# Lower halves of every second weight chunk made by accumulating DMAs from GpSimd instead of VectorE subtractions

## Chip, core and metric

One core of one Trainium2 chip. The metric is the time of one execution in microseconds (us), device time, as the median of several runs. The engines are named TensorE (PE), VectorE (DVE), ScalarE (ACT), GpSimd (POOL) and SyncE (SP).

## What is computed

Two transformer-like blocks on one sequence of 512 tokens, 1024 wide, in float32. The first block has two layers, each with a convolution branch, a retention branch and a windowed attention branch; the second has a spatial gate, a gated linear recurrence and a feed-forward part:

```python
def reference(x, ...):
    x = first_block(x, ...)                 # 2 x hybrid_layer
    return second_block(x, ...)

def hybrid_layer(x, ...):
    h = rms_norm(x, norm_g)
    z = h @ w_in
    y_conv = conv_module(...) @ w_conv_out
    y_ret = retention_branch(...) @ w_ret_out
    y_attn = window_attention_branch(...) @ w_attn_out
    merged = g[:, :, 0] * y_conv + g[:, :, 1] * y_ret + g[:, :, 2] * y_attn
    return x + merged @ w_out

# at the end of second_block
hid = silu(h1 @ w_ffn_gate) * (h1 @ w_ffn_up)
ffn = hid @ w_ffn_down
h = layer_norm(ALPHA * h1 + ffn + ple, ...)
```

Nearly all of the arithmetic is products of activations with weight matrices.

## The kernel before

Every product with a weight matrix is made of three: each operand is split into an upper part `hi` (rounded to the fp32r type that PE reads) and a lower part `lo`, the float32 value less its upper part. `mm3` (lines 173 to 177) then adds up upper times upper, upper times lower and lower times upper in one PSUM tile, so one block of 128x128 weights costs three matmuls, on lines 175, 176 and 177. In the products that hold the weights still (`fm`, line 179) the weights' lower part is first read by the third of the three.

The weights lie in DRAM in the order in which they are used, in 502 chunks of 128x1024 float32 (512 KB, 8 blocks each; `w`, `NCHUNK`). `take` (line 158) hands out the blocks. Before it hands out a block of chunk c it has everything up to chunk c+2 split (`WB` = 3, line 162). For each chunk `_split_next` (line 135) writes three steps into the program:

- the chunk's load into a tile `raw`, issued by SP (`_load_raw`, line 131),
- its upper part, a cast `hi<-raw` on ACT (line 152; the first three chunks on line 150),
- its lower part, a subtraction `lo<-raw,hi` on DVE (line 153),

and then the load of the next chunk, three ahead. `raw`, `hi` and `lo` each have three buffers that go round. So the cast for chunk c waits until PE has read the last block of chunk c-3 out of `hi`, the lower part until PE has read `lo` of chunk c-3, and the load of chunk c+3 until the lower part of chunk c is made, which is the last to read `raw`. ACT, DVE, SP and PE take their instructions in the order of the program; that order is set by a scheduler when the program is built.

Eleven chunks in `HOLD` (306 to 311 and 399 to 403) go another way: they are split into slots of their own, by `split` (line 206) on lines 208 and 209.

Most chunks serve matmuls of 512 columns. In two places they serve less. The down projection of the feed-forward part, at the end of the program, runs over the two halves of the tokens, one after the other (`HALVES`, lines 1306 to 1317), 256 columns each, and takes its 44 chunks (458 to 501) for 22 x 8 blocks twice. The first projection of the second block (`tmproj` with `halves`, lines 961 and 191) takes chunks 312 to 319 for two token tiles at a time.

Steps that the text names: the feed-forward part (lines 1296 to 1303) evicts with a tanh on ACT (line 1299, recorded on line 226) and two operations on DVE (line 216), and splits the product on lines 208 and 209.

Of the kernel before, what the change touches and what calls it, by code (L numbers as in the profile page):

```python
# [10 lines left out]
F32 = mybir.dt.float32  # L11
F32R = mybir.dt.float32r
I32 = mybir.dt.int32
AF = mybir.ActivationFunctionType
ALU = mybir.AluOpType
# [55 lines left out]
class Kern:  # L71
# [63 lines left out]
    def _split_next(self):  # L135
        c = self.nsplit
        if c >= NCHUNK:
            return
        while self.nraw <= c:
            self._load_raw()  # L140
        raw = self.raw.pop(c)
        if c in HOLD:
            parts = [self.split(raw[:, i * 512:i * 512 + 512]) for i in range(2)]
            self.hi[c], self.lo[c] = [x[0] for x in parts], [x[1] for x in parts]
        else:
            h = self.hp.tile([128, 1024], F32R, tag="hi", name=f"hi{c}")
            l = self.lp.tile([128, 1024], F32R, tag="lo", name=f"lo{c}")
            if c in self.first:
                with self.tc.issue_after(self.first[c].ins):
                    self.A.copy(h, raw)  # L150
            else:
                self.A.copy(h, raw)  # L152
            self.V.tensor_tensor(out=l, in0=raw, in1=h.bitcast(F32), op=ALU.subtract)  # L153
            self.hi[c], self.lo[c] = h, l
        self.nsplit += 1
        self._load_raw()
# [1362 lines left out]
```

## Time and profile before

| what | value |
|---|---|
| median of 2 runs | 3081.85 us (3081.53 to 3082.16) |
| the profiled execution | 3081.39 us |
| its span, first to last instruction | 3079.6 us |
| granted TensorE clock, mean | 0.997 |
| PE / PEld / DVE / ACT / POOL busy | 98% / 82% / 69% / 38% / 0% |
| DMA moved | 281.77 MB, 28.0% of the 16 DMA engines on the queue of SP |

Busy time is the time in which an engine runs an instruction; matmuls are pipelined, so a busy PE need not run at its peak. PEld are the weight loads of PE, which run beside its matmuls. DMAs are issued by an engine's sequencer and carried by 16 DMA engines; "to landing" is from the issue to the update of the semaphore that tells of it. In a timeline row the first number is the start in us from the span's start, the second the duration in us, and in brackets stands how long the engine sat idle before it, and what released it.

### The profile page before, as it was taken

Reading aid. Unit: us, or ns where it says so; the run is one execution under the profiler, and the core shown is the slowest. Engines: PE = TensorE matmul, PEld = TensorE weight load, DVE = VectorE, ACT = ScalarE, POOL = GpSimd, SP = SyncE. Lnnn points to the kernel's source line nnn. Section 1 sums busy time; section 2 is a strip of 40 time slices with the busy share of each in tenths; the row PEclk is TensorE's granted clock in tenths of the full one; section 3 lists DMA queues with packets and bytes.
Section 4 is the critical chain, followed back from the end, with each engine's and each line's share of the span. In section 5 each row is a group of like instructions: output and inputs, shape, how many; then the busy total and the mean of one; then the engine's idle time right before and its main releaser. Section 6 shows DMA issues by size and latency. Waiting matters only on the chain.

```text
span 3079.6 us, 37755 instructions
## 1 busy us (share of the span) xinstructions
PE 3033.3 (98%) x14728; PEld 2510.4 (82%) x14728; DVE 2128.3 (69%) x3934; ACT 1156.2 (38%) x1822; POOL 0.2 (0%) x4
## 2 busy tenths in 40 slices
PE   9999999999999999999999999999999999999998
PEld 7777888887888877788888788887888888788898
DVE  8687997877344677889787754388876656744356
ACT  5545223334233454532333423243543333322233
POOL 0000000000000000000000000000000000000000
PEclk9999999999999999999999999999999999999999
DMA  4121322221323322123222132333222223132354
GB/s 163 62 76 49 97 83 81 76 83 62 103 96 130 117 69 68 56 84 95 76 76 76 63 102 96 107 118 131 89 83 69 69 78 121 62 96 96 97 170 138
DMA packets 82114, 281.77 MB, mean 91 GB/s; under 512 B 9232, under 2 KB 11536, under 8 KB 81808
## 3 DMA queue, kind: packets, MB, share of 16 engines
q1 hardware_dynamic: 81936, 279.37, 28.0%
q8 instruction: 115, 1.88, 0.3%
q14 instruction: 63, 0.52, 0.1%
HBM read 275.14 MB, written 4.19 MB: 91 GB/s over the span
## 4 chain that ended last, share of the span: by engine, by line
PE 91%; DVE 6%; ACT 2%; issue 1%; DMA 0%; SPq 0%; ACTq 0%; DVEq 0%
PE pm L175 20%; PE pm L177 20%; PE pm L176 20%; PE pa L175 7%; PE pa L177 7%; PE pa L176 7%; DVE s L213 1%; PE pi L773 1%; PE pa L794 1%; DVE lo L153 1%; PE pi L175 1%; PE pi L177 1%; PE pi L176 1%; ACT s L226 1%; PE pa L1094 1%
## 5 line engine op out<-in xcount | busy, mean ns | idle before, releaser
L175 PE MATMUL pm<-s,hi 128*128 128x512 f32 x2912 | 1140.7, 392 | 1.8 <-ACT s L226 1.8
L176 PE MATMUL pm<-s,hi 128*128 128x512 f32 x2912 | 1139.5, 391 | 0.0
L177 PE MATMUL pm<-s,lo 128*128 128x512 f32 x2912 | 1135.9, 390 | 0.0
L152 ACT CAST hi<-raw 128x1024 fp32r<-128x1024 f32 x488 | 513.5, 1052 | 1365.9 <-PE pm L176 801.2
L153 DVE TENSOR_TENSOR lo<-raw,hi 128x1024 fp32r<-128x1024 f32 x491 | 599.8, 1222 | 450.2 <-ACT hi L152 442.4
L175 PEld LDWEIGHTS pm<-s,hi 128*128 128x128 f32 x2912 | 547.0, 188 | 119.3 <-issue 3.5
L177 PEld LDWEIGHTS pm<-s,lo 128*128 128x128 f32 x2912 | 547.2, 188 | 114.7 <-issue 2.2
L176 PEld LDWEIGHTS pm<-s,hi 128*128 128x128 f32 x2912 | 547.3, 188 | 113.0 <-issue 1.7
L216 DVE SCALAR_TENSOR_TENSOR s<-s,m,s 128x497 f32<-128x497 f32 (+14 forms) x480 | 356.3, 742 | 11.2
L216 DVE SCALAR_TENSOR_TENSOR s<-s,pm 128x512 f32<-128x512 f32 x186 | 127.2, 684 | 208.9 <-PE pm L177 208.5
L175 PE MATMUL pa<-hi,s 128*128 128x512 f32 x576 | 228.4, 397 | 11.7 <-ACT hi L150 6.7
L176 PE MATMUL pa<-lo,s 128*128 128x512 f32 x576 | 227.3, 395 | 0.0
L177 PE MATMUL pa<-hi,s 128*128 128x512 f32 x576 | 226.9, 394 | 0.0
L208 ACT CAST s<-s 128x512 fp32r<-128x512 f32 x192 | 115.6, 621 | 192.5 <-DVE s L216 146.7
L213 DVE TENSOR_TENSOR s<-s,s 128x512 f32<-128x512 f32 (+2 forms) x284 | 168.5, 610 | 3.2 <-ACT s L226 0.5
L209 DVE TENSOR_TENSOR s<-s,s 128x512 fp32r<-128x512 f32 x192 | 128.5, 687 | 28.7 <-ACT s L208 27.9
L175 PEld LDWEIGHTS pa<-hi,s 128*128 128x128 f32 x576 | 109.1, 190 | 36.4 <-ACT hi L150 6.7
L176 PEld LDWEIGHTS pa<-lo,s 128*128 128x128 f32 x576 | 109.2, 190 | 22.6 <-DVE lo L153 0.8
L177 PEld LDWEIGHTS pa<-hi,s 128*128 128x128 f32 x576 | 109.0, 189 | 22.0
L175 PE MATMUL pa<-s,hi 128*128 128x256 f32 (+1 forms) x408 | 122.2, 300 | 1.0 <-ACT s L1277 1.0
L177 PE MATMUL pa<-s,lo 128*128 128x256 f32 (+1 forms) x408 | 122.1, 300 | 0.0
L176 PE MATMUL pa<-s,hi 128*128 128x256 f32 (+1 forms) x408 | 121.5, 298 | 0.0
(143 smaller groups left out, 2905.1 us busy)
## 6 DMA issues: line engine op xcount, KB each, us to landing
raw<-w SPq DMA_DIRECT2D x502, 512.0 KB, 3.4
s<-xT SPq DMA_DIRECT2D x16, 256.0 KB, 5.3
xd<-s SPq DMA_DIRECT2D x8, 256.0 KB, 2.0
s<-xd SPq DMA_DIRECT2D x8, 256.0 KB, 4.8
out<-s SPq DMA_DIRECT2D x16, 128.0 KB, 1.8
ckt<-ck SPq DMA_DIRECT2D x1, 1344.0 KB, 6.4
s<-c_b_v SPq DMA_DIRECT2D x2, 256.0 KB, 3.9
s<-c_b_i SPq DMA_DIRECT2D x2, 256.0 KB, 3.9
```

The source lines that it names most:

```text
L152: self.A.copy(h, raw)
L153: self.V.tensor_tensor(out=l, in0=raw, in1=h.bitcast(F32), op=ALU.subtract)
L175: T.matmul(out, lhsT=lh, rhs=rh, start=start, stop=False)
L176: T.matmul(out, lhsT=lh, rhs=rl, start=False, stop=False)
L177: T.matmul(out, lhsT=ll, rhs=rh, start=False, stop=stop)
L208: self.A.copy(h, src)
L209: self.V.tensor_tensor(out=l, in0=src, in1=h.bitcast(F32), op=ALU.subtract)
L213: return self.V.tensor_tensor(out=out, in0=a, in1=b, op=op)
L216: return self.V.scalar_tensor_tensor(out=out, in0=a, scalar=s, in1=b, op0=op0, op1=op1)
L226: return self.A.activation(out, a, f, bias=bias, scale=scale, **kw)
L773: T.transpose(ps[:, i * 128:i * 128 + 128], pr[i][:, x * 128:x * 128 + 128], self.ck("ident"))
L794: T.matmul(ps[:, 0:w], lhsT=a[hs, ns], rhs=b[hs, j0:j1], start=first, stop=last)
```

## The change

For every odd chunk above 5 the subtraction on DVE goes. ACT writes the negated upper part into the tile `lo` (a copy with scale -1), and GpSimd then issues a DMA that adds `raw` to it in place: -hi + raw. Even chunks, chunks up to 5 and the held chunks stay as they are. There are 242 such odd chunks. Line numbers behind line 153 move on by five: what stood on line 153 is line 158 in the new file, the three matmuls are on 180, 181 and 182, `act` is on 231, and the new DMA is on 156.

```diff
             else:
                 self.A.copy(h, raw)
-            self.V.tensor_tensor(out=l, in0=raw, in1=h.bitcast(F32), op=ALU.subtract)
+            if c > 5 and c % 2:
+
+                self.act(l, h.bitcast(F32), AF.Copy, scale=-1.0)
+                self.nc.gpsimd.dma_start(out=l, in_=raw, accum_op=ALU.add)
+            else:
+                self.V.tensor_tensor(out=l, in0=raw, in1=h.bitcast(F32), op=ALU.subtract)
             self.hi[c], self.lo[c] = h, l
```

The feed-forward part, ACT, from the cast of chunk 436 on, before (`pm` is a PSUM tile, `s` a slot of 128x512; the numbers tell buffers apart):

```order
L152 CAST hi_22691<-raw_22588 128x1024
L208 CAST s_22686<-s_22651 128x512
L152 CAST hi_22726<-raw_22624 128x1024
L226 ACTIVATE s_22721<-pm_22690 128x512
L152 CAST hi_22762<-raw_22659 128x1024
L208 CAST s_22757<-s_22722 128x512
```

The same place now:

```order
L152 CAST hi_22900<-raw_22796 128x1024
L213 CAST s_22895<-s_22859 128x512
L152 CAST hi_22935<-raw_22832 128x1024
L231 ACTIVATE s_22930<-pm_22899 128x512
L231 ACTIVATE lo_22936<-hi_22935 128x1024
L152 CAST hi_22972<-raw_22868 128x1024
```

The negated copy of odd chunk 437 stands behind one eviction that follows its cast.

The down projection, ACT, from the cast of chunk 470 on, before:

```order
L152 CAST hi_23852<-raw_23763 128x1024
L152 CAST hi_23885<-raw_23793 128x1024
L152 CAST hi_23915<-raw_23826 128x1024
L152 CAST hi_23945<-raw_23856 128x1024
L152 CAST hi_23978<-raw_23889 128x1024
```

and now:

```order
L152 CAST hi_24078<-raw_23988 128x1024
L152 CAST hi_24111<-raw_24018 128x1024
L231 ACTIVATE lo_24112<-hi_24111 128x1024
L152 CAST hi_24142<-raw_24052 128x1024
L152 CAST hi_24172<-raw_24082 128x1024
L231 ACTIVATE lo_24173<-hi_24172 128x1024
```

Each odd chunk's copy follows its cast at once. On POOL, where nothing stood in the program's body, the transfers of this stage follow one another:

```order
L156 DMA lo_24048<-raw_23957 128x1024
L156 DMA lo_24112<-raw_24018 128x1024
L156 DMA lo_24173<-raw_24082 128x1024
L156 DMA lo_24237<-raw_24146 128x1024
L156 DMA lo_24329<-raw_24210 128x1024
```

The second and the third belong to the two odd chunks of the piece of ACT above. Besides, the scheduler puts some 500 of the 14152 matmuls of PE, mostly those of attention and retention, a few places earlier or later.

## Rows read from the trace of the kernel before

**Rows 1.** The page's head: span, and busy time of each engine.
```profile
span 3079.6 us, 37755 instructions
PE 3033.3 (98%) x14728; PEld 2510.4 (82%) x14728; DVE 2128.3 (69%) x3934; ACT 1156.2 (38%) x1822; POOL 0.2 (0%) x4
```
**Rows 2.** The chain that ended last, by engine and by line.
```profile
PE 91%; DVE 6%; ACT 2%; issue 1%; DMA 0%; SPq 0%; ACTq 0%; DVEq 0%
...
by line: PE pm L175 20.3%; PE pm L177 20.1%; PE pm L176 20.1%; PE pa L175 7.2%; PE pa L177 7.2%; PE pa L176 7.2%; DVE s L213 1.4%; PE pi L773 1.3%; PE pa L794 1.2%; DVE lo L153 1.2%; PE pi L175 1.0%; PE pi L177 1.0%; PE pi L176 1.0%; ACT s 
```
**Rows 3.** Timeline of ACT in the feed-forward part.
```profile
2703.98 1.05 ACT L152 CAST hi<-raw 128x1024 fp32r<-128x1024 f32 x1 [3.90 <-PE pm L176]
2704.94 0.61 ACT L208 CAST s<-s 128x512 fp32r<-128x512 f32 x1
2709.47 1.05 ACT L152 CAST hi<-raw 128x1024 fp32r<-128x1024 f32 x1 [3.91 <-issue]
2710.43 0.58 ACT L226 ACTIVATE s<-pm 128x512 f32<-128x512 f32 x1
```
**Rows 4.** Timeline of DVE at the same place.
```profile
2705.07 1.23 DVE L153 TENSOR_TENSOR lo<-raw,hi 128x1024 fp32r<-128x1024 f32 x1 [0.17 <-ACT hi L152]
```
**Rows 5.** Groups of instructions, whole span: busy us, mean ns, idle time before.
```profile
L152 ACT CAST hi<-raw 128x1024 fp32r<-128x1024 f32 x488 | 513.5, 1052 | 1365.9 <-PE pm L176 801.2
L153 DVE TENSOR_TENSOR lo<-raw,hi 128x1024 fp32r<-128x1024 f32 x491 | 599.8, 1222 | 450.2 <-ACT hi L152 442.4
```
**Rows 6.** Stretches: length, busy us and number of casts (line 152), clock, DMA share.
```profile
740.00:990.00 250.00, 48.51 (x46) 1.00 0.32 106
...
1750.00:2000.00 250.00, 47.46 (x46) 1.00 0.30 98
...
2160.00:2270.00 110.00, 20.21 (x20) 1.00 0.30 95
...
2660.00:2920.00 260.00, 50.56 (x48) 1.00 0.30 96
```
**Rows 7.** Timeline of ACT in the down projection.
```profile
2952.72 1.05 ACT L152 CAST hi<-raw 128x1024 fp32r<-128x1024 f32 x1 [1.83 <-PE pa L176]
2955.60 1.05 ACT L152 CAST hi<-raw 128x1024 fp32r<-128x1024 f32 x1 [1.83 <-PE pa L176]
```
**Rows 8.** Stretches of feed-forward and down projection, all engines.
```profile
core 0: us, PE busy (x) PEld busy (x) DVE busy (x) ACT busy (x) POOL busy (x), PEclk, DMA share, GB/s
...
2700.00:2740.00 40.00, 40.00 (x178) 33.15 (x177) 16.98 (x20) 11.01 (x15) 0.00 (x0) 1.00 0.30 93
2935.00:2985.00 50.00, 50.00 (x416) 49.79 (x415) 26.69 (x36) 19.15 (x21) 0.00 (x0) 1.00 0.58 179
```
**Rows 9.** Timeline of ACT in the first projection of the second block.
```profile
2074.69 1.05 ACT L152 CAST hi<-raw 128x1024 fp32r<-128x1024 f32 x1 [1.28 <-issue]
...
2077.41 1.06 ACT L152 CAST hi<-raw 128x1024 fp32r<-128x1024 f32 x1 [1.08 <-PE pa L177]
```
**Rows 10.** DMA, whole span: queue of SP, and the loads of chunks.
```profile
q1 hardware_dynamic: 81936, 279.37, 28.0%
...
raw<-w SPq DMA_DIRECT2D x502, 512.0 KB, 3.4
```
**Rows 11.** DMA from 2925 to 3052 us, the down projection.
```profile
q1 hardware_dynamic: 7052, 22.53, 55.1%
...
raw<-w SPq DMA_DIRECT2D x40, 512.0 KB, 4.2
```
**Rows 12.** DMA, whole span: the quickest store of 256 KB, the slowest load.
```profile
xd<-s SPq DMA_DIRECT2D x8, 256.0 KB, 2.0
...
vkt<-vk SPq DMA_DIRECT2D x1, 300.0 KB, 6.7
```
**Rows 13.** Stretches of first attention and of the second block's start, all engines.
```profile
55.00:190.00 135.00, 132.85 (x666) 105.35 (x665) 94.91 (x260) 67.44 (x150) 0.00 (x0) 1.00 0.21 66
2030.00:2160.00 130.00, 121.14 (x610) 101.75 (x610) 111.24 (x275) 47.90 (x74) 0.00 (x0) 0.97 0.32 102
```

## Prediction

> **What bounds the kernel now.** I read the page's head first. TensorE (PE) is busy 3033.3 us of a span of 3079.6, at a granted clock of 1.00, the upper of its two levels, 2.4 GHz, in the stretches read below [rows 1, 8]. So 46 us is all that any change of the other engines' work can win back, 1.5% of the span. The chain that ended last says the same: 91% of it lies on PE, 6% on VectorE (DVE), 2% on ScalarE (ACT), and the lower parts formed by DVE (line 153) hold 1.2% of it, 37 us [rows 2]. DVE's work is not what sets the end. What matters is whether the new way of making a lower part arrives before PE wants it.
>
> That is read from the rhythm of the chunks. The three tiles `hi` and the three tiles `lo` go round: the cast that fills chunk c may start when PE has read the last block of chunk c-3, and PE wants chunk c two chunks later. In the feed-forward stage ACT's casts stand 5.44 us apart and wait for PE, as the first of the rows names it [rows 3], so the time between a release and its need is 2 x 5.44 = 10.88 us. Of it the kernel before uses 2.3 us: a cast of 1.05 us, then DVE's subtraction of 1.22 us, which begins 0.04 us after the cast ends [rows 3, 4]. More than 8 us lie unused. The pace is not the same everywhere. Four stretches run at about 5.44 us a chunk and hold 46, 46, 20 and 48 casts, 160 in all and so 80 odd chunks [rows 6]; in the down projection at the end, chunks stand 2.88 us apart [rows 7], because there every chunk feeds matmuls of 256 columns only. PE has no gap in that stage, and its DMA share is 0.58, against 0.30 in the feed-forward stage [rows 8]. The allowance there is 2 x 2.88 = 5.76 us. The first projection of the second block has a like place: its first 8 chunks (312 to 319) serve two token tiles at a time, 12 matmuls each, and the casts stand 2.7 us apart, an allowance of 5.44 us [rows 9].
>
> **The change, part by part.** Removed: 242 subtractions on DVE of 1.22 us, 295 us of 2128 [rows 1, 5]. Added on ACT: 242 negated copies of a 128x1024 tile. No row shows one; a cast of the same tile on the same engine takes 1.05 us [rows 5], and I take that: 254 us, which brings ACT from 38% to 45% of the span. It stays far from being the bound. Added on GpSimd (POOL): 242 accumulating transfers of 512 KB, from one tile in SBUF to another. Nothing else is queued on POOL, so a waiting transfer holds up only its own chunk. PE waits for the landing at the third matmul of the chunk, and all of PE's work stands behind that wait.
>
> The price of the transfer decides, and no row of before shows one. The nearest row is the load of `raw`, as many bytes over as many partitions: 3.4 us from issue to landing. All loads together keep the 16 DMA engines busy for 28.0% of the span, 862 us for 279 MB, so 1.62 us for 512 KB [rows 10]. An accumulating transfer has to read `raw` and the old `lo`, so I count the engines' part twice: 3.4 + 1.6 = 5.0 us. In the down projection loads land after 4.2 us, since they queue behind each other [rows 11]; there I take 4.2 + 1.6 = 5.8 us. The ends are 2.0 us, which half the bytes take out of SBUF, and 11.4 us, the slowest landing in the trace (6.7 us for 300 KB) scaled to 512 KB [rows 12]. I keep to the value near the raw load, because size, shape and pace of issue are its own.
>
> The Trainium skill, Collectives: The Full Stack, section "The bandwidth ceiling: the fold count and why AG ≠ RS ≠ AR", says that an add inside a transfer costs no time of its own, but that its second read halves the rate; no run here shows that yet. Were the second read free, the two transfers would take 3.4 and 4.2 us, and by the formula below the time would be 3088 us.
>
> Now the wait. From the release to the landing it takes a cast 1.05, a copy 1.05, two hand-overs of about 0.1 us (an estimate; 0.04 is seen from ACT to DVE) and the transfer: 2.3 us plus t. In the feed-forward stage an eviction of 0.58 us stands between cast and copy [rows 3], so 2.9 plus t. If this exceeds the allowance, PE stands still in front of that chunk. The release for the next odd chunk comes just before this standstill, so the standstill lengthens the next one's allowance, and over two odd chunks the excess is paid once. Loss for each odd chunk: (chain - allowance) / 2.
> - Four dense stretches: 2.9 + 5.0 = 7.9 against 10.88 us. Nothing is lost; the cover is 3 us and is gone at t = 8.0. Stages with attention or retention between the chunks have more.
> - Down projection, 22 odd chunks: (2.3 + 5.8 - 5.76) / 2 = 1.17 us each, 26 us.
> - First projection of the second block, 4 odd chunks: (2.3 + 5.0 - 5.44) / 2 = 0.93 us each, 4 us.
> As a check on the second: the 40 loads in the window keep the DMA engines busy 55.1% of 127 us, 70 us or 1.75 us each [rows 11]. The 22 new transfers at twice that add 77. 147 us of DMA work do not fit in 127, so the stage must grow by 20 us at least if both reads count in full; 26 agrees.
>
> A side effect is the refill of `raw`. It now waits for the landing, on SP, with later loads queued behind it. In the down projection the buffer comes free 8.1 us after the release instead of 2.3; the load lands at 12.3; the cast that wants it could start at 11.0 and is 1.3 us late. That chunk is even, made by DVE in 2.3 us, and wanted at 16.7: hidden, with 2 us to spare.
>
> DVE's relief: half of its 37 us on the chain would be 18 us. But PE rarely waits: in the stretch where DVE is fullest beside an idle PE, 2030 to 2160, PE is idle 9 us while DVE is busy 111 of 130 [rows 13]. I take 4 us off. Against it stand ACT's copies ahead of its exponentials in attention, where PE idles 2 us in 135 [rows 13], and some 500 matmuls that the scheduler has moved: 2 us added.
>
> Sum: 26 + 4 - 4 + 2 = 28 us on the profiled execution's own 3081.4 us (1.8 us around its span). It lies 0.5 us under the median of the runs, 3081.85, so 3109 us, 0.9% more.
>
> The Trainium skill, DMA: Bandwidth & Descriptors, section "Latency and other measured facts", speaks against the change: the first byte of a transfer issued by GpSimd takes about 1 us, of one issued by SP about 0.6. No row here shows either. By it t would be 0.4 us longer, the 26 odd chunks would lose 0.2 us more each, and the time would be 3114 us.
>
> **Rivals.**
> 1. The transfer is slow, and the ring of three buffers closes everywhere. Point of decision: at t = 7.4 the down projection loses (2.3 + 8.2 - 5.76) / 2 x 22 = 52 us and the first projection 9, together the 2% of 62 us; above t = 8.0 the 80 dense odd chunks join. At t = 10 the three places lose 81, 14 and 80 x (12.9 - 10.88) / 2 = 81 us, together 176: 3257 us. At the upper end, 11.4, they lose 96, 17 and 137 us: 3331. For it: nothing in the trace shows descriptors written by GpSimd, or a transfer that reads, adds and writes the same tile. Against it: the DMA engines are busy 28% only, and POOL does nothing else.
> 2. All is hidden and DVE's relief counts in full: t at 3.4 us or less, loss about 0, 18 us off: 3064 us. For it: transfers out of SBUF land in 2.0 us [rows 12]. Against it: the few gaps of PE, and a second read.
> 3. ACT becomes late: the copy before an eviction holds a PSUM tile, and PE waits for it. With 1 us in each of some 22 odd chunks of the two attention stages, 22 us more: 3131 us. Against it: ACT idles 1366 us in front of its casts [rows 5], so it has slack wherever a cast waits for PE.
> That the change does not do what it says is ruled out by the order: 242 copies on ACT, 242 transfers on POOL, 242 subtractions fewer on DVE.
>
> **How the numbers follow.** Forecast with t from 3.4 to 7.4: 0.50. Rival 1: 0.37. Rival 2: 0.09. Rival 3: 0.04. Faster by over 2% (about what a measurement tells from no change) would need under 3020 us, more than all of PE's idle time: 0.01. Slower by over 2%, above 3143.5, is rival 1: 0.37. Within: 0.62. The range leaves out the fastest part of rival 2 and the slowest part of rival 1: 3070 to 3290 us. The forecast's own range is 3085 to 3143.
>
> **What would show it.** Right: landings of `lo` at about 5 us, PE gaps before the third matmul (line 182 of the new file) in the last 150 us of the span and hardly any between 2660 and 2920, DVE at 59%, ACT at 45%. Wrong: landings above 7.4 us, waits for the transfer in the feed-forward stage, or casts that wait for `raw`.

## The result and the profile after

The changed kernel took 3111.19 us (median of 2 runs, 3109.51 to 3112.87) against 3081.85 before: 1.0095 times as long, 95% interval 1.0078 to 1.0112. The prediction was 3109. Its profiled execution, the slower of the two runs, has a span of 3110.9 us, 31.3 more than the span of before [rows 1].

The head of the page of the changed kernel:

```profile
span 3110.9 us, 38558 instructions
PE 3039.8 (98%) x14728; PEld 2519.3 (81%) x14728; DVE 1862.2 (60%) x3692; ACT 1386.2 (45%) x2060; POOL 209.2 (7%) x246
```

DVE lost 266 us of work and ACT gained 230, and neither shows in the span. The chain that ended last, by engine and by line:

```profile
PE 88%; DMA 4%; DVE 4%; ACT 2%; issue 2%; SPq 0%; POOLq 0%; POOL 0%; ACTq 0%
...
by line: PE pm L180 20.5%; PE pm L181 20.3%; PE pm L182 20.3%; PE pa L180 6.2%; PE pa L181 6.2%; PE pa L182 6.2%; DMA lo<-raw 2.3%; issue 1.8%; DMA raw<-w 1.4%; ACT s L231 1.3%; PE pi L778 1.0%; PE pa L799 0.9%; PE pi L180 0.9%; PE pi L182 
```

DMA stood at 0% before [rows 2]; now the new transfers hold 2.3% of the chain and the loads 1.4%. DVE fell from 6% to 4%. The groups that answer to [rows 5]:

```profile
L152 ACT CAST hi<-raw 128x1024 fp32r<-128x1024 f32 x488 | 513.6, 1053 | 1265.4 <-PE pm L181 1028.7
L158 DVE TENSOR_TENSOR lo<-raw,hi 128x1024 fp32r<-128x1024 f32 x249 | 304.1, 1221 | 244.7 <-ACT hi L152 236.4
L156 POOL DMA_DIRECT2D lo<-raw x242 | 209.0, 864 | 2875.9 <-ACT lo L231 2270.1
L231 ACT ACTIVATE lo<-hi 128x1024 fp32r<-128x1024 f32 x242 | 254.9, 1053 | 2.6
L182 PE MATMUL pa<-s,lo 128*128 128x256 f32 (+1 forms) x408 | 126.8, 311 | 21.5 <-DMA lo<-raw 21.4
L181 PE MATMUL pa<-lo,s 128*128 128x512 f32 x576 | 228.5, 397 | 5.2 <-DMA lo<-raw 4.8
```

The negated copy costs 1.05 us, what the cast costs. Issuing a transfer keeps POOL busy 0.86 us. Transfers ended the idle time of two groups of matmuls: 21.4 us before the third matmul of the down projection, and 4.8 us before the second matmul (line 181) of the products whose weights move, which is where the first projection of the second block reads the lower part. What the transfers cost the DMA engines, over the whole span (queues: packets, MB, share of 16 engines; issues: median us to landing):

```profile
q1 hardware_dynamic: 81936, 279.37, 26.9%
q0 software_dynamic: 34848, 126.89, 20.7%
...
raw<-w SPq DMA_DIRECT2D x502, 512.0 KB, 3.6
lo<-raw POOLq DMA_DIRECT2D x242, 512.0 KB, 4.4
```

and from 2925 to 3085 us, the down projection:

```profile
q1 hardware_dynamic: 7138, 22.82, 43.7%
q0 software_dynamic: 3024, 11.01, 35.3%
...
raw<-w SPq DMA_DIRECT2D x40, 512.0 KB, 4.2
lo<-raw POOLq DMA_DIRECT2D x22, 512.0 KB, 5.8
```

So a transfer lands after 4.4 us, and after 5.8 in the down projection. Of the 16 engines it takes 20.7% of 3110.9 us, divided by 242: 2.66 us, where 512 KB of a load take 26.9% x 3110.9 x 0.524 / 279.37 = 1.57.

Where the 31 us went is read by stretches (columns as in [rows 8]):

```profile
2660.00:2920.00 260.00, 260.00 (x1149) 215.29 (x1148) 86.83 (x114) 97.50 (x120) 20.75 (x24) 1.00 0.52 144
2920.00:3097.00 177.00, 154.80 (x1141) 148.40 (x1139) 58.38 (x115) 78.53 (x92) 18.93 (x22) 0.94 0.75 199
2941.20:2946.50 5.30, 5.26 (x31) 5.26 (x32) 0.13 (x1) 1.05 (x1) 0.63 (x1) 0.68 0.82 181
3000.30:3007.10 6.80, 6.80 (x34) 6.67 (x33) 1.77 (x3) 1.46 (x2) 0.00 (x0) 0.50 0.85 227
3031.00:3037.80 6.80, 3.74 (x17) 3.74 (x18) 0.84 (x2) 2.10 (x2) 0.67 (x1) 0.50 0.82 260
```

The feed-forward stretch is untouched: PE busy 260 of 260 us at clock 1.00, with 24 transfers in it. The down projection is not: PE idles 22 us, and the granted clock falls to 0.50, its lower level of 1.2 GHz, in parts of it. Those parts begin beside gaps of PE. The trace's record of the clock has 20.5 us of them between the stage's start and 3097 us; the mean of 0.94 over 177 us fits it. Before, this stage ran at 1.00 [rows 8].

One such wait, in the order in which it came about (timelines of ACT, POOL and PE):

```profile
2990.01 1.05 ACT L152 CAST hi<-raw 128x1024 fp32r<-128x1024 f32 x1 [1.83 <-PE pa L181]
2991.09 1.06 ACT L231 ACTIVATE lo<-hi 128x1024 fp32r<-128x1024 f32 x1
...
2992.44 0.86 POOL L156 DMA_DIRECT2D lo<-raw  x1 [7.18 <-DVE s L218]
...
2999.21 0.39 PE L182 MATMUL pa<-s,lo 128*128 128x256 f32 x1 [2.45 <-DMA lo<-raw]
```

PE releases the tile, the cast starts at 2990.01, the copy follows, the transfer is issued at 2992.44 (2.43 us after the cast's start; the prediction had 2.3), 0.29 us after the copy's end, and PE starts the third matmul only at 2999.21, after 2.45 us of standing still. At 3000.30 the clock is at 0.50. The profile names a step of DVE as what released the transfer; it lies 0.29 us behind the copy here as in nearly all cases, so the copy is what it follows.

The longest of these waits came about in another way (ACT, then PE):

```profile
3022.38 1.05 ACT L152 CAST hi<-raw 128x1024 fp32r<-128x1024 f32 x1 [0.77 <-PE pa L181]
3023.33 2.51 ACT L231 ACTIVATE s<-s,vkt 128x256 f32<-128x256 f32 x6
3025.74 1.04 ACT L231 ACTIVATE lo<-hi 128x1024 fp32r<-128x1024 f32 x1
...
3034.06 0.58 PE L182 MATMUL pa<-s,lo 128*128 128x256 f32 x1 [4.94 <-DMA lo<-raw]
```

This is chunk 485, where the output of the first half of the tokens is written. Six activations of that output stand between its cast and its copy, which starts 3.36 us after the cast instead of 1.08, and the transfer takes 6.9 us, among the stores of the output and loads.

To place the loss I read the start of the cast of the same chunk in each trace, changed minus before:

| from, to | loss (+) or gain (-), us | predicted |
|---|---|---|
| start to chunk 312 | -5.4 | |
| first projection of the second block, 312 to 330 | +6.1 | +4 |
| chunk 330 to 458 | -3.4 | |
| down projection, 458 to the end | +34.0 | +26 |
| all | +31.3 | +28 |

The parts outside the two short places sum to -8.8; the prediction had -4 and +2 there, -2 together.

### The profile page after: what moved, and what is told of

It is laid out like the page before. It is cut to its first block, busy times and chain, and to the rows that moved or that the text cites. A ratio compares the mean times of both kernels' runs of the same rounds, so it can differ in the third digit from the quotient of the medians.

```text
span 3110.9 us, 38558 instructions
## 1 busy us (share of the span) xinstructions
PE 3039.8 (98%) x14728; PEld 2519.3 (81%) x14728; DVE 1862.2 (60%) x3692; ACT 1386.2 (45%) x2060; POOL 209.2 (7%) x246
## 3 DMA queue, kind: packets, MB, share of 16 engines
q1 hardware_dynamic: 81936, 279.37, 26.9%
q0 software_dynamic: 34848, 126.89, 20.7%
## 4 chain that ended last, share of the span: by engine, by line
PE 88%; DMA 4%; DVE 4%; ACT 2%; issue 2%; SPq 0%; POOLq 0%; POOL 0%; ACTq 0%
PE pm L180 20%; PE pm L181 20%; PE pm L182 20%; PE pa L180 6%; PE pa L181 6%; PE pa L182 6%; DMA lo<-raw 2%; DMA raw<-w 1%; ACT s L231 1%; PE pi L778 1%; PE pa L799 1%; PE pi L180 1%; PE pi L182 1%; PE pi L181 1%; DVE s L218 1%
## 5 line engine op out<-in xcount | busy, mean ns | idle before, releaser
L158 DVE TENSOR_TENSOR lo<-raw,hi 128x1024 fp32r<-128x1024 f32 x249 | 304.1, 1221 | 244.7 <-ACT hi L152 236.4
L156 POOL DMA_DIRECT2D lo<-raw x242 | 209.0, 864 | 2875.9 <-ACT lo L231 2270.1
L231 ACT ACTIVATE lo<-hi 128x1024 fp32r<-128x1024 f32 x242 | 254.9, 1053 | 2.6
L182 PE MATMUL pa<-s,lo 128*128 128x256 f32 (+1 forms) x408 | 126.8, 311 | 21.5 <-DMA lo<-raw 21.4
```

The costliest lines, as they stand in the source:

```text
L156: self.nc.gpsimd.dma_start(out=l, in_=raw, accum_op=ALU.add)
L182: T.matmul(out, lhsT=ll, rhs=rh, start=False, stop=stop)
L231: return self.A.activation(out, a, f, bias=bias, scale=scale, **kw)
```

## The experiments

Each kernel is the changed one with the edit shown. Medians stand beside those of the kernel before from the same chip.

**Transfers only outside the two short places.**

```diff
-            if c > 5 and c % 2:
+            if 5 < c < 456 and c % 2 and not 311 < c < 324:
```

> The change without its transfers for chunks 312 to 323 and from 456 on, where chunks follow each other in 2.7 to 2.9 us. If the loss is the chain of an odd chunk (cast, copy, transfer) against the time of two chunks, it is gone and only what DVE was relieved of remains: about 3072 us, 10 us faster than before. If the copies on ACT or the moved order of the matmuls cost the time, 214 of 242 chunks still pay: about 3107 us.

Measured: 3075.81 us against 3081.77, ratio 0.9977 (0.9968 to 0.9986).

```profile
span 3071.4 us, 38453 instructions
...
PE 3024.3 (98%) x14728; PEld 2508.3 (82%) x14728; DVE 1895.4 (62%) x3721; ACT 1357.2 (44%) x2031; POOL 184.2 (6%) x217
```

Its 213 transfers take 4.4 us each to land, and PE waits for none. The whole loss lies in the two short places. What remains is a gain of 6 us by the medians, put down to the relief of DVE; the profiled execution, the fastest of the ten, has 8.2 us less of span than the kernel before. It builds up in steps of 1 to 3 us in the parts with attention and recurrence. It does not lie in the idle time of PE, which is 47 us here and was 46 before: PE's busy time is 9.0 us shorter [rows 1]. This version is faster than both kernels, by 0.2% than the kernel before.

**Transfers only in the down projection.**

```diff
-            if c > 5 and c % 2:
+            if c > 457 and c % 2:
```

> The change for the 22 odd chunks from 458 on alone, the down projection. By the chain against two chunks nearly the whole loss stands there: about 3116 us, 34 us slower than before, a little more than the full change, since DVE's relief elsewhere is missing. If each transfer costs alike: 3085 us.

Measured: 3116.07 against 3081.77, ratio 1.0106 (1.0092 to 1.0119). The 22 transfers of this stage alone cost at least about as much as the whole change. That they cost more, as the missing relief would have it, is not clear of noise: the intervals overlap.

**Transfers only in the first projection of the second block.**

```diff
-            if c > 5 and c % 2:
+            if 311 < c < 324 and c % 2:
```

> Only the first projection of the second block: odd chunks 313 to 323 by transfer, six of them, everything else as before the change. Theory A: the place costs 9 us, as it did in the changed kernel where one standstill of 4.8 us in front of a lower part and half clock after it showed there: 3088 to 3092. Theory B, the prediction's 4 us: 3084 to 3087. Theory C, that standstill needs the other transfers before it or the moved order: 3081 to 3083.

Measured: 3088.59 against 3081.29, ratio 1.0022 (1.0013 to 1.0032): theory A, at the lower end of its range. Of the six transfers, those of chunks 317 and 319 make PE wait (timeline of PE):

```profile
2070.03 0.50 PE L181 MATMUL pa<-lo,s 128*128 128x512 f32 x1 [1.64 <-DMA lo<-raw]
...
2082.95 0.79 PE L181 MATMUL pa<-lo,s 128*128 128x512 f32 x1 [4.40 <-DMA lo<-raw]
```

In the changed kernel the chain of waits, in order of time, tells how such a wait comes about:

```profile
2056.95 7.14 DMA lo<-raw
2064.15 3.50 DMA raw<-w
2070.05 7.68 DMA lo<-raw
```

Two transfers took 7.1 and 7.7 us there instead of 4.4, and between them a load of `raw`, issued right at the first one's landing, lies on the chain: the refill that the first one had held up. Then PE waited 4.8 us at 2077.78. The timeline of ACT shows why the second transfer, that of chunk 319, began so late:

```profile
2064.36 1.05 ACT L152 CAST hi<-raw 128x1024 fp32r<-128x1024 f32 x1 [1.53 <-PE pa L182]
2065.31 1.31 ACT L231 ACTIVATE s<-s,vkt 128x256 fp32r<-128x256 f32 x3
2067.75 1.05 ACT L152 CAST hi<-raw 128x1024 fp32r<-128x1024 f32 x1 [1.13 <-DMA raw<-w]
2068.70 1.06 ACT L231 ACTIVATE lo<-hi 128x1024 fp32r<-128x1024 f32 x1
```

Its copy stands behind three activations and the cast of chunk 320, and that cast waited 1.13 us more for the held-up load. So the copy starts 4.34 us after its own cast instead of 1.08 as in most of the down projection.

**The copies of ACT, with an addition on DVE in place of the transfer.**

```diff
-                self.nc.gpsimd.dma_start(out=l, in_=raw, accum_op=ALU.add)
+                self.V.tensor_tensor(out=l, in0=raw, in1=l.bitcast(F32), op=ALU.add)
```

> ACT's negated copies stay for all 242 odd chunks, but DVE adds raw to them in place of the transfer. The chain is then 1.05 + 1.05 + 1.22 us, under 5.44 everywhere: 3082 us, within 4 us of before. If the copies on ACT, or the order that comes with them, were the cost: about 3100 us or more. If it lies under 3078, part of the gain outside the two short places comes from the order and not from DVE's relief.

Measured: 3085.40 against 3081.77, ratio 1.0010 (1.0001 to 1.0019). DVE does as much as before (2129.2 us), ACT as much as after (1391.1). Copies and moved order cost 2 to 4 us. The first experiment has the copies too (213 of 242) and lies 9.6 us lower, which points to DVE's fewer instructions as the source of its gain. The matmuls stand in different orders in the two versions, so a share of the order is not excluded.

**Twice the transfer.** Each transfer is issued twice on a copy scaled by -2, so the lower part comes out doubled.

```diff
-                self.act(l, h.bitcast(F32), AF.Copy, scale=-1.0)
+                self.act(l, h.bitcast(F32), AF.Copy, scale=-2.0)
                 self.nc.gpsimd.dma_start(out=l, in_=raw, accum_op=ALU.add)
+                self.nc.gpsimd.dma_start(out=l, in_=raw, accum_op=ALU.add)
```

> Each transfer is done twice, one after the other, onto a copy scaled by -2, so that the lower part of these chunks comes out doubled. From landing to landing the cost is then twice 4.4 us, and twice 5.8 in the down projection. By the chain against two chunks: down projection (2.3 + 11.6 - 5.76) / 2 x 22 = 90 us, first projection 11, and now also the dense stretches, (2.9 + 8.8 - 10.88) / 2 = 0.41 us for each of 80 to 127 odd chunks, 33 to 52 us, less 8 of relief: 3208 to 3227 us, with waits of PE in the feed-forward part. If only the load on the DMA engines counted, the down projection alone would grow, by some 60 us in all: about 3140 us, and no waits in the feed-forward part.

Measured: 3483.91 against 3081.77, ratio 1.1309 (1.1274 to 1.1344). The expected time was far too low. The dense stretches join, as the prediction's rule of the allowance says, and with the rhythm that it says (timeline of ACT, feed-forward part):

```profile
2945.18 1.05 ACT L152 CAST hi<-raw 128x1024 fp32r<-128x1024 f32 x1 [7.84 <-PE pm L182]
2950.62 1.05 ACT L152 CAST hi<-raw 128x1024 fp32r<-128x1024 f32 x1 [3.80 <-PE pm L182]
...
2956.06 1.05 ACT L152 CAST hi<-raw 128x1024 fp32r<-128x1024 f32 x1 [2.95 <-PE pm L182]
2961.50 1.05 ACT L152 CAST hi<-raw 128x1024 fp32r<-128x1024 f32 x1 [3.87 <-PE pm L182]
...
2972.16 1.05 ACT L152 CAST hi<-raw 128x1024 fp32r<-128x1024 f32 x1 [8.17 <-PE pm L182]
```

Casts stand 5.44 us apart, then once 10.66: one standstill for two odd chunks. Its size was the miss. The median landing rose to 5.0 us, and of the two transfers of one chunk in this stretch one took 4.4 us and the other, beside a load of `raw`, 7.4. Many standstills, not all, have a stretch at clock 0.50 beside them; the clock's record has 244 us of them in the span. PE's weight loads waited for transfers in three groups:

```profile
PEld pm L183 <- DMA lo<-raw: 204.9, 82, 5.3
...
PEld pa L183 <- DMA lo<-raw: 64.4, 17, 8.0
PEld pa L182 <- DMA lo<-raw: 61.5, 23, 5.7
```

331 us of waits and half of 225 us (244 less the 19 that the kernel before has) make 443; the span grew by 400. The sum is too high: PE stands still in part of the time at 0.50, which counts that part twice (18 us), and the relief of DVE comes off. What is left of the difference is open.

**No accumulation.** The odd chunks' upper part is set to zero and `raw` is moved by a plain transfer, so it is the lower part alone.

```diff
+            elif c > 5 and c % 2:
+                self.act(h, raw, AF.Copy, scale=0.0)
...
-                self.nc.gpsimd.dma_start(out=l, in_=raw, accum_op=ALU.add)
+                self.nc.gpsimd.dma_start(out=l, in_=raw)
```

> For the same odd chunks the cast is scaled by 0, so that the upper part is zero and the whole value goes into the lower part; the transfer then is a plain one of raw without the addition, at the same place behind the same copy. The weights' split is left out for these chunks. If the second read makes the transfer long (328 ns for a 4096 byte packet of the added ones, 159 ns for a load's), it lands in about 3.0 us instead of 4.4; the down projection then loses (2.3 + 3.8 - 5.76) / 2 x 22 = 4 us in place of some 34, and with 10 us of relief the time is 3072 to 3080 us. If the way of issue makes it long, it lands in 4.4 us as before and the time stays at 3111 us.

Measured: 3092.34 against 3082.27, ratio 1.0035 (1.0021 to 1.0049), between the two expectations.

```profile
q0 software_dynamic: 34848, 126.89, 11.1%
...
lo<-raw POOLq DMA_DIRECT2D x242, 512.0 KB, 2.9
```

Without the add a transfer takes 11.1% x 3091.1 / 242 = 1.42 us of the DMA engines instead of 2.66, and lands after 2.9 us instead of 4.4 (3.7 instead of 5.8 in the down projection). So what the accumulation adds is real, and two thirds of the loss go with it; that it is a second read is the prediction's reading, which this run does not tell from another cost of adding. The rest stays because PE's weight loads still wait 11.5 us in the down projection and 3.9 in the first projection. The longest wait, 5.2 us, is again that of chunk 485, with its copy 3.36 us after its cast; its transfer and two loads, issued between 3012.6 and 3014.8, all land after some 6 us, near 3019 to 3021.

**Four tiles `raw`.** Two slots fewer make room.

```diff
-        self.rp = pool("rp", WB)
+        self.rp = pool("rp", 4)
```

> Four tiles raw instead of three, hi and lo as before (three), two slots of 128x512 fewer to make room. The load of chunk c+3 then goes into the tile that chunk c-1 has left, so it no longer waits for the transfer of chunk c. Theory A, the refill of raw is a bound of its own in the down projection: six chunks use the ring of three twice, with 3 x (4.2 load + 2.3) + 3 x (4.2 load + 2.3 + 5.8 transfer) = 57 us over 3 tiles, 18.9 us, where PE needs 6 x 2.88 = 17.3; with four tiles 14.2. The stage then loses some 20 to 25 us instead of 34, and the whole takes 3096 to 3103. Theory B, the refill is hidden, as the prediction had it: 3109 to 3114, the stage still loses over 30. If the transfers beside the loads fill the DMA engines, B's number comes out too, with landings of lo above 6 us.

Measured: 3109.20 against 3081.29, ratio 1.0090 (1.0075 to 1.0105): theory B. The waits for the lower part in the down projection stay:

```profile
PEld pa L182 <- DMA lo<-raw: 28.4, 19, 3.8
```

The refill of `raw` is not what costs in the down projection with three tiles `hi` and `lo`: the waits grew from 25.1 to 28.4 us. In the first projection the cast of chunk 320 no longer waits for `raw`, but the copy of chunk 319 still stands behind it and the activations, 3.74 us after its own cast, and PE waits 4.6 us.

**Transfers only for every second odd chunk of the down projection.**

```diff
-            if c > 5 and c % 2:
+            if c > 457 and c % 4 == 1:
```

> Only every second odd chunk of the down projection (461, 465, ..., 501: 11 transfers), everything else as before the change. Theory A, the prediction's formula: a single odd chunk among three that DVE makes has no earlier standstill to lengthen its allowance, so it pays the whole excess, 2.3 + 5.8 - 5.76 = 2.3 us, or 1.5 us if its transfer takes 5.0 with fewer loads beside it: 17 to 26 us, 3099 to 3108. Theory B, what costs is the ring of raw and the sum of DMA work: 44 loads x 1.75 + 11 transfers x 2.7 = 107 us fit in 127, and the ring of raw has 4 x 4.2 + 4 x 2.3 + 5.8 = 31.8 us over 3 tiles, 10.6, for four chunks of 11.5: loss under 8 us, 3084 to 3090.

Measured: 3102.18 against 3081.29, ratio 1.0064 (1.0047 to 1.0081): theory A. Eleven transfers instead of 22 still cost half, though now the DMA engines have room and a transfer lands after 4.5 us:

```profile
q1 hardware_dynamic: 7056, 22.55, 41.5%
q0 software_dynamic: 1584, 5.77, 18.6%
...
lo<-raw POOLq DMA_DIRECT2D x11, 512.0 KB, 4.5
```

The excess of one chain, 2.3 + 4.5 - 5.76 = 1.04 us, times 11 is 11.5 us; the waits are these:

```profile
PE pa L182 <- DMA lo<-raw: 12.5, 9, 6.7
...
PEld pa L182 <- DMA lo<-raw: 14.8, 10, 6.9
```

The sum comes near the 12.5 us of PE's matmuls, but only in part for the formula's reason. Eight of the nine waits are 1.2 us at most, as the formula says; one of 6.7 us is more than half of the sum. It is that of chunk 485: eight activations stand before its copy, which starts 4.16 us after the cast, and its transfer takes 7.7 us beside the stores of the output.

**Those 11 transfers with four tiles `hi` and `lo`.** Chunks are split one earlier; four slots fewer.

```diff
-            if c > 5 and c % 2:
+            if c > 457 and c % 4 == 1:
...
-        self.hp = pool("hp", WB)
-        self.lp = pool("lp", WB)
+        self.hp = pool("hp", 4)
+        self.lp = pool("lp", 4)
...
-        while self.nsplit <= min(c + WB - 1, NCHUNK - 1):
+        while self.nsplit <= min(c + 3, NCHUNK - 1):
```

> The 11 transfers of the run with every second odd chunk of the down projection (461, 465, ..., 501), with four tiles hi and four lo, chunks split one earlier and four slots fewer, raw still three. Theory A, the prediction's: what a lower part may take is set by the ring of hi and lo. With four tiles it is 3 x 2.88 = 8.64 us, more than the 2.3 + 4.5 = 6.8 that the chain takes there, and the ring of raw has 10.6 us of work for four chunks of 11.5: the stage loses under 5 us, where it lost 18 with three tiles, and the whole takes 3085 to 3090 (the kernel before with four tiles: 3084.85). Theory B, transfer and loads disturb each other however early the chunk is split, as in the run with all 22 odd chunks and four tiles, which lost 40 us here: the stage loses 12 us or more, 3097 to 3105.

Measured: 3088.49 against 3083.48, ratio 1.0018 (1.0009 to 1.0028): theory A. Of the waits for a transfer in the stage one is left, 1.7 us; the copy of chunk 485 follows its cast at once here. The same transfers, 4.8 us to landing, cost 18 us with three tiles and 5 with four. (Casts come one chunk earlier in this kernel, so its stage is compared with the kernel before in the same form, below.) The 40 us that the expectation names for 22 transfers become 35 by that comparison.

**All 242 transfers with four tiles `hi` and `lo`,** and the kernel before in that form. `raw` stays at three; the other lines of the edit are those of the run above.

```diff
-        self.hp = pool("hp", WB)
-        self.lp = pool("lp", WB)
+        self.hp = pool("hp", 4)
+        self.lp = pool("lp", 4)
```

> The full change with four buffers of hi and lo instead of three and the split one chunk further ahead (raw stays at three; 66 slots in place of 70 make the room). The allowance becomes three chunks: 8.6 us in the down projection against a chain of 2.3 + 5.8 = 8.1. By the chain nearly all of the 34 us there and the 9 us in the first projection go, and DVE's relief stays: 3070 to 3085 us. If the load on the DMA engines made the loss, it stays: about 3105 us.

> The kernel before with four buffers of hi and lo, split one chunk further ahead, and 66 slots: the control for the run before. Its chain of 2.3 us had 5.4 us or more, so a fourth buffer is worth nothing to it: 3082 us within 5. If it gains as much as the changed kernel does, the gain there is not that of the chain.

Measured: 3128.39 against 3082.27, ratio 1.0153 (1.0137 to 1.0169), and 3084.85 for the kernel before in that form. The expectation missed by 43 us or more. In the down projection ACT now waits for the ring of `raw` (waits of ACT from 2920 us on):

```profile
ACT hi L152 <- DMA raw<-w: 62.8, 27, 7.3
```

In the changed kernel that row reads 8.6 us in 4 waits, in the kernel before 8.5. Three loads with odd chunks behind them and three with even ones take 3 x (4.4 + 2.3 + 6.1) + 3 x (4.4 + 2.3) = 58.5 us over three tiles, 19.5 us for six chunks, where PE takes 17.3. For 44 chunks that is 16 us, less than half of the 35 that the stage lost. Loads and transfers land later here too: 4.4 and 6.1 us. The longest wait of PE, 8.6 us, is once more at chunk 485, whose copy starts 8.1 us after its cast, behind activations and a cast that waits for `raw`. So the ring of `raw` is part of the cause by the waits; how much of it, and how much is the load on the DMA engines, is not shown. All three rings at four tiles were not tried. Some 8 us more are lost outside the stage, with two waits of PE for DVE of 3.8 us that the control lacks; they were not followed up.

**All chunks, odd and even, outside the short places.**

```diff
-            if c > 5 and c % 2:
+            if 5 < c < 456 and not 311 < c < 324:
```

> Every chunk, even ones too, goes over the transfer, but not chunks 312 to 323 and those from 456 on. In the dense stretches the chain is 2.9 + 4.4 = 7.3 us against 10.88, so nothing is lost, and DVE is relieved of twice as much: 3062 to 3070 us. If DVE's relief is exhausted by the odd chunks alone, it stays at about 3075 us. If the ring does close with every chunk in it, since the refill of raw waits for each landing, the time rises above 3082.

Measured: 3079.48 against 3082.27, ratio 0.9994 (0.9985 to 1.0002). With twice the relief of DVE (1662.9 us busy) no gain is left that is clear of noise; by the medians it is 2.8 us, about half of that with odd chunks alone. Transfers now land after 5.5 us and loads after 4.2; which of the small waits took the gain back stays open.

## Why the prediction came out right, and where its terms were off

**The mechanism holds, and that the number came so near is in part luck.** A ring of three tiles gives the lower part two chunks' time; where chunks are dense that is 10.88 us and covers the chain, where they feed short matmuls it is 5.8 and does not. No wait from 2660 to 2920 us, the loss gone without the two places, the loss in half with half of the transfers, and all but gone with a fourth tile at 11 transfers: these four say the same. The fourth tile with 22 transfers did not help, so there something else binds. Run with a doubled transfer, the dense chunks joined and paid once for two odd chunks, as the formula has it, though at a much higher price.

**The price of the transfer.** Predicted 5.0 us, and 5.8 in the down projection; measured 4.4 and 5.8. Of the first, what the add costs was right (4.4 with it, 2.9 without, 1.5 us against 1.6) and the base too long: 2.9 instead of the load's 3.4. In the down projection both were off and cancel: 3.7 without the add and 2.1 for it, where the prediction had 4.2 and 1.6. The Trainium skill, Collectives: The Full Stack, section "The bandwidth ceiling: the fold count and why AG ≠ RS ≠ AR", has the second read halve the rate, and the DMA engines' time agrees: 2.66 us with the add, 1.42 without. The Trainium skill, DMA: Bandwidth & Descriptors, section "Latency and other measured facts", would have made GpSimd's transfers 0.4 us later than SP's, by an estimate from its two figures. No run shows the first byte, and the plain transfer landed earlier than a load, not later, though it reads SBUF and the load DRAM.

**The down projection, 26 us.** The formula gave the sum of the waits well: PE's weight loads waited 25.1 us for transfers.

```profile
PEld pa L182 <- DMA lo<-raw: 25.1, 17, 5.1
```

The longest of them, 5.1 us, has a cause that the formula leaves out: it lets the copy follow its cast at once, and at chunk 485 the copy came 2.3 us later. And the stage lost 34.0. The term that is missing from this step is the clock, which fell beside some of the waits. Time at 0.50 costs half of itself, and with it the stage's loss adds up in five runs:

| run | waits of PEld, us | at clock 0.50, us | waits + half | loss of the stage |
|---|---|---|---|---|
| changed kernel | 25.1 | 20.5 | 35.3 | 34.0 |
| only the down projection | 27.6 | 17.1 | 36.1 | 35.7 |
| four tiles `raw` | 28.4 | 3.4 | 30.1 | 31.1 |
| every second odd chunk | 14.8 | 6.8 | 18.2 | 18.4 |
| no accumulation | 11.5 | 6.8 | 14.9 | 14.5 |

(The loss is the time from the cast of chunk 458 to the end less that of before. The time at 0.50 leaves out the last stretch, which lies behind the products in every run, the kernel before too. With four tiles `hi` and `lo` the stage lost 40.7 us with 22 transfers and 10.2 with 11, the kernel before in that form 5.4; so 35.3 and 4.8 are the transfers'. Where PE stands still at 0.50, that time is counted twice: in the changed kernel PE ran in 17.5 of the 20.5 us, and with half of those the sum is 33.8.) What decides when the clock falls is not shown: with four tiles `raw` the waits were as long in sum, and it stood at 0.50 for 3.4 us only.

**The check by DMA work** (the stage must grow by 20 us at least) was right in size for a wrong reason. A transfer takes 2.66 us of the engines, not twice 1.75; loads and transfers together are 79% of 160 us, 126 us, and would just have fit in the 127. With 11 transfers the engines have room, and the stage still loses 18.4 us, though the wait of chunk 485 is 6.9 of them.

**The refill of `raw`** was called late but hidden. In the down projection it was: a fourth tile made no wait shorter in sum (28.4 us against 25.1), and the 2.9 us less that the stage lost go with a clock that stood less at 0.50. In the first projection it cost a cast 1.13 us and, through the order on ACT, a copy; a fourth tile took that wait away and the wait of PE stayed.

**The first projection, 4 us.** It cost 6 in the changed kernel and 7.3 alone. The place was right, the shape wrong: not 0.93 us in each of four chunks, but one long wait, when two transfers took over 7 us beside loads and the second one's copy came 3.3 us late, with a stretch at half clock beside it.

**The relief of DVE, 4 us, and 2 us for ACT and the order.** The second was about right (2 to 4 by the run with the addition on DVE). The relief was sized too small: outside the short places the changed kernel's profile gained 8.8 us net, the version without them 6 by the medians, so some 8 to 12 before the cost of the copies. Reading it from the gaps of PE in two stretches [rows 13] missed it, since the gain does not lie in PE's gaps. The prediction's bound for any such gain, PE's idle time of 46 us, leaves out this part as well.

So two terms that were too small on the loss side (8 and 2 us) and one on the gain side (7 us) nearly cancel: 31 against 28. That is luck.

**The rivals.** The slow transfer did not come: the median of 5.8 us stands below its point of 7.4, though single transfers of this stage took up to 8.2. Full relief with all hidden did not come, but the version without the short places shows the hidden part. A late ACT costs 2 to 4 us at most by itself, as the run with the addition on DVE shows. Joined to a transfer it costs more: the longest waits, at chunks 319 and 485, have a copy that came 3.3 and 2.3 us late. A version with these two copies moved up was not run.

## What to carry to other kernels

Work out the time between a buffer's release and its need for each stage, not for the kernel; a slower but freer way of making an operand belongs only where that allowance covers its whole chain, as here for the 213 of 242 chunks outside the two places. Look at what stands between the steps of that chain on their engine, at the changes of stage above all. Lengthen the ring that binds only after working out what the next ring, here the one of the staging tile, would then allow. Count a standstill of PE at more than its length, since the clock can fall beside it.

## What was not expected of the hardware

- PE's granted clock was 0.50 for 20.5 us of the down projection, beside or right after waits of 1.6 to 4.9 us; without waits for transfers, in the kernel before, it ran at 1.00 up to the last products. This was about 9 of the 34 us. Waits of 2.2 and 1.65 us had no such stretch beside them.
- An accumulating transfer from SBUF to SBUF holds the DMA engines 1.9 times as long as a plain one (2.66 and 1.42 us for 512 KB) and keeps POOL busy 0.86 us at its issue instead of 0.53.
- Its landing differs with the place: 4.4 us in the dense stretches, 5.8 among the loads of the down projection, over 7 for two that met loads in the first projection.
